# Batched 64x64 matmul: `a` regrouped by its load DMA instead of by a VectorE copy

## The chip, the cores and the metric

The kernel runs on one core of one Trainium2 chip, as one launch with one program. The metric is the device time of that core in microseconds (us), lower is better; each version's time is the median of several runs. The trace comes from one profiled execution, whose own time stands beside the median below.

## The reference

```python
def setup_inputs():
    return {
        "a": np.random.randn(1024, 64, 64).astype(np.float32),
        "b": np.random.randn(1024, 64, 64).astype(np.float32),
    }

def reference(a, b):
    return np.matmul(a, b).astype(np.float32)
```

These are 1024 independent products of a 64x64 matrix `a[i]` with a 64x64 matrix `b[i]`, float32 in and out. Inputs are 16.78 MB each, the output is 16.78 MB.

## The kernel before, in words

The batch is cut into 16 tiles of T = 64 matrices. A matrix of a tile has the index t, h (0 to 3), g (0 to 15). All operands are cast from float32 to bf16 by the DMA that loads them, and all DMAs, loads and stores, are issued from GpSimd (POOL), in one queue and in the order of the code.

- **Load of `a`** (`load_a`, line 59): one DMA a tile fills `a_sb` [128, 4, 8, 64]. Partition (g, mp) holds 8 consecutive rows of `a` (v = 0 to 7) for each h. In DRAM these 8 rows are one run of 8 x 64 float32 = 2 KB; in SBUF they land as one run of 512 bf16 = 1 KB. There are 128 x 4 = 512 such runs a tile.
- **Load of `b`** (`load_b`, line 66): four DMAs a tile, one for each h, put `b` onto the diagonal of a block-diagonal operand `b_bd` [128, 16, 4, 128]: h picks 32 partitions and one of 4 column blocks. Each run is 128 float32 = 512 B in DRAM and 256 B in SBUF, 512 runs a DMA. The zeros off the diagonal are written once, by four VectorE memsets at the start (lines 70 and 76), one for each of the NB = 4 buffers.
- **Regrouping of `a`** (line 88): a VectorE copy reorders `a_sb` (h outside v) to `a_bf` (v outside h), so that the columns (h, k) of one row index v lie together, `a_cols` [128, 8, 256].
- **Transposes** (line 98): 16 TensorE transposes a tile of 128x128 slices of `a_cols` (every second column, by u) into PSUM tiles `at_ps`, and four VectorE copies (line 102) from there to `at_sb`.
- **Products** (line 114): 64 matmuls a tile with 32 columns of `at_sb` as weights and 256 columns of `b_bd` moving, accumulated over u in four PSUM tiles `o_ps`. Each `o_ps` is copied to `o_sb` by ScalarE (line 126) for even gq and by VectorE (line 128) for odd gq.
- **Store** (line 130): one DMA a tile writes 1 MB of `o_sb` (8 KB contiguous a partition) to `out`, where each partition's data are 16 separate runs of 128 float32 = 512 B.

What sets the order: `load_a` and `load_b` run AHEAD = 3 tiles in front of the products, and the store of tile t stands on POOL behind the loads of tile t+3. `a_sb` has 4 buffers, `b_bd` 4, `o_sb` 3, the two PSUM pools 4 each. The DMAs take eight completion semaphores in turn, so that in the program each DMA waits on POOL until the DMA eight places before it has landed, besides its own data waits. A tile issues 6 DMAs: one for `a`, four for `b`, one store.

Of the kernel before, what the change touches and what calls it, by code (L numbers as in the profile page):

```python
# [1 line left out]

# [5 lines left out]

fp32 = mybir.dt.float32
bf16 = mybir.dt.bfloat16  # L10


@with_exitstack
def kernel(
    ctx: ExitStack,
    tc: tile.TileContext,
    a: bass.AP,
    b: bass.AP,
    out: bass.AP,
):  # L20

    nc = tc.nc
    B, M, K = a.shape
    _, _, N = b.shape
    assert (M, K, N) == (64, 64, 64) and B % 64 == 0

    T = 64
    n_t = B // T
    AHEAD = 3
    NB = 4

    a_v = a.rearrange("(t h g) (mp v) k -> t (g mp) h (v k)", h=4, g=16, v=8)
    b_v = b.rearrange("(t h g) (kp u) n -> t h kp g (u n)", h=4, g=16, u=2)
    o_v = out.rearrange("(t hq g4) (mo w) n -> t (g4 mo) hq (w n)", hq=16, g4=4, w=2)

    consts = ctx.enter_context(tc.tile_pool(name="consts", bufs=1))  # L40
    a_pool = ctx.enter_context(tc.tile_pool(name="a_pool", bufs=NB))
    at_pool = ctx.enter_context(tc.tile_pool(name="at_pool", bufs=3))
    o_pool = ctx.enter_context(tc.tile_pool(name="o_pool", bufs=3))
    t_psum = ctx.enter_context(
        tc.tile_pool(name="t_psum", bufs=4, space=bass.MemoryType.PSUM)
    )
    o_psum = ctx.enter_context(
        tc.tile_pool(name="o_psum", bufs=4, space=bass.MemoryType.PSUM)
    )

    b_tiles = []
    for i in range(NB):
        b_bd = consts.tile([128, 16, 4, 128], bf16, name=f"b_bd{i}")
        b_tiles.append(b_bd)
    a_tiles = {}

    def load_a(t):
        a_sb = a_pool.tile([128, 4, 8, 64], bf16, name="a_sb")
        nc.gpsimd.dma_start(  # L59
            out=a_sb[:].rearrange("p h v k -> p h (v k)"), in_=a_v[t]  # L60
        )
        a_tiles[t] = a_sb

    def load_b(t):
        for h in range(4):
            nc.gpsimd.dma_start(  # L66
                out=b_tiles[t % NB][32 * h : 32 * h + 32, :, h, :], in_=b_v[t, h]
            )

    nc.vector.memset(b_tiles[0][:], 0.0)  # L70
    load_a(0)
    load_b(0)
    identity = consts.tile([128, 128], bf16)
    make_identity(nc, identity)
    for i in range(1, NB):
        nc.vector.memset(b_tiles[i][:], 0.0)  # L76
    for t in range(1, AHEAD):
        load_a(t)
        load_b(t)

    for t in range(n_t):
        if t + AHEAD < n_t:
            load_a(t + AHEAD)
            load_b(t + AHEAD)
        a_sb = a_tiles.pop(t)
        b_bd = b_tiles[t % NB]
        a_bf = at_pool.tile([128, 8, 4, 64], bf16, name="a_bf")
        nc.vector.tensor_copy(  # L88
            a_bf[:], a_sb[:].rearrange("p h v k -> p v h k")
        )  # L90
        a_cols = a_bf[:].rearrange("p v h k -> p v (h k)")

        at_sb = at_pool.tile([128, 2, 2, 128, 4], bf16, name="at_sb")
        for w in range(2):
            at_ps = t_psum.tile([128, 4, 2, 128], bf16, name="at_ps")
            for vo in range(4):
                for u in range(2):
                    nc.tensor.transpose(  # L98
                        at_ps[:, vo, u, :], a_cols[:, 2 * vo + w, u::2], identity[:]
                    )  # L100
            for u in range(2):
                nc.vector.tensor_copy(  # L102
                    at_sb[:, w, u, :, :],
                    at_ps[:, :, u, :].rearrange("p vo q -> p q vo"),
                )

        o_sb = o_pool.tile([128, 4, 4, 2, 64], fp32, name="o_sb")
        for gq in range(4):
            o_ps = o_psum.tile([128, 2, 4, 64], fp32, name="o_ps")
            for w in range(2):  # L110
                for u in range(2):
                    for g4 in range(4):
                        g = 4 * gq + g4
                        nc.tensor.matmul(  # L114
                            o_ps[32 * g4 : 32 * g4 + 32, w, :, :],
                            at_sb[:, w, u, 8 * g : 8 * g + 8, :].rearrange(
                                "p mp vo -> p (mp vo)"
                            ),
                            b_bd[:, g, :, 64 * u : 64 * u + 64],
                            start=(u == 0),  # L120
                            stop=(u == 1),
                        )
            dst = o_sb[:, :, gq, :, :]
            src = o_ps[:].rearrange("p w h n -> p h w n")
            if gq % 2 == 0:
                nc.scalar.copy(dst, src)  # L126
            else:
                nc.vector.tensor_copy(dst, src)  # L128

        nc.gpsimd.dma_start(  # L130
            out=o_v[t], in_=o_sb[:].rearrange("p h q w n -> p (h q w n)")
        )


# [1 line left out]
_INS = ['a', 'b']  # L136
_OUTS = [((1024, 64, 64), 'float32')]


# [23 lines left out]
```

## Time and profile before

| | |
|---|---|
| median of 3 runs | 146.64 us (145.87 to 147.1) |
| the profiled execution's own time | 145.87 us |
| its span in the trace | 144.1 us |
| PE busy (with weight loads apart) | 74.8 us, 52% (50.7 us) |
| DVE busy | 86.1 us, 60% |
| ACT busy | 19.2 us, 13% |
| POOL busy, issuing DMAs for nearly all of it | 74.5 us, 52% |
| VectorE regrouping copies (line 88) | 16 of 724 ns |

How to read it: the page gives busy time of each engine, then the span in 40 slices (a digit is a busy share in tenths, 9 for 90% or more), then the DMA queues with packets, bytes and the time that packets took as a share of 16 DMA engines' span (over 100% where packets of one engine overlap). The bytes of a load are counted as they land in SBUF, in bf16, so a 2 KB run of `a` is a packet of 1 KB. Then comes the chain of work that ended last, then the groups of instructions: line, engine, operation, out<-in, count, busy us and mean ns of one, then the idle time of the engine before them and what ended it. A DMA-issuing instruction on POOL is shown as DMA_DIRECT2D; its duration is that of the issuing, not that of the transfer.

### The profile page before, as it was taken

How to read it: one execution, taken by the hardware profiler on the slowest of the kernel's cores; microseconds unless marked ns; L12 is line 12 of the kernel's file. 1: busy time of each engine (PE TensorE's matmuls, PEld its weight loads, DVE VectorE, ACT ScalarE, POOL GpSimd, SP SyncE). 2: the span in 40 equal slices, each digit the busy share in tenths (PEclk: the TensorE clock that was granted, in tenths of full speed). 3: DMA queues.
4: the chain of work that ended last, by engine and by line, in shares of the span. 5: the costliest groups of instructions: out<-in, count | busy, mean ns of one | idle time of the engine just before them, and what ended most of it. 6: DMA issues, size and time to landing. Idle time of an engine off the chain costs nothing.

```text
span 144.1 us, 2993 instructions
## 1 busy us (share of the span) xinstructions
PE 74.8 (52%) x1280; PEld 50.7 (35%) x1280; DVE 86.1 (60%) x116; ACT 19.2 (13%) x33; POOL 74.5 (52%) x102
## 2 busy tenths in 40 slices
PE   0000089786462617558484648829286484856300
PEld 0000057464342414345443325527153354433200
DVE  5777989997776436373565656373463735656300
ACT  3000002231130200202011030301103020110300
POOL 6457881961935627375555738255471655620110
PEclk9999999999999975865559555595557755586855
DMA  1999999999999999999999999999999999999873
GB/s 8 182 177 179 179 178 179 259 187 186 328 209 282 247 228 297 198 321 201 297 234 252 278 210 315 191 309 224 268 256 216 287 207 301 223 284 367 285 232 105
DMA packets 46604, 33.74 MB, mean 234 GB/s; under 512 B 34304, under 2 KB 42496, under 8 KB 46592
## 3 DMA queue, kind: packets, MB, share of 16 engines
q0 software_dynamic: 46592, 33.56, 128.4%
q8 instruction: 10, 0.16, 0.4%
q14 instruction: 2, 0.02, 0.0%
HBM read 33.55 MB, written 16.78 MB: 349 GB/s over the span
## 4 chain that ended last, share of the span: by engine, by line
DMA 52%; DVE 16%; issue 10%; PE 8%; POOL 7%; POOLq 1%; ACT 1%; DVEq 0%
DMA a_sb<-in_a_dram 52%; DVE b_bd L76 7%; PE at_ps L98 5%; POOL out_dram L130 4%; DVE at_sb L102 4%; PE o_ps L114 3%; DVE a_bf L88 3%; DVE b_bd L70 2%; POOL b_bd L66 2%; POOLq L158 1%; ACT o_sb L126 1%; DVE o_sb L128 0%; DVEq L88 0%
## 5 line engine op out<-in xcount | busy, mean ns | idle before, releaser
L66 POOL DMA_DIRECT2D b_bd<-in_b_dram x64 | 42.8, 673 | 42.8 <-DMA a_sb<-in_a_dram 20.4
L114 PE MATMUL o_ps<-b_bd,at_sb 128*32 128x256 bf16 x1024 | 52.7, 359 | 15.2 <-DVE at_sb L102 7.8
L102 DVE COPY at_sb<-at_ps 128x512 bf16<-128x512 bf16 x64 | 39.7, 682 | 11.3 <-PE at_ps L98 11.3
L98 PE MATMUL at_ps<-identity,a_bf 128*128 128x128 bf16 x256 | 22.5, 257 | 44.6 <-DVE a_bf L88 44.6
L114 PEld LDWEIGHTS <-at_sb 128*32 128x32 bf16 x1024 | 31.6, 120 | 33.7 <-DVE at_sb L102 27.8
L128 DVE COPY o_sb<-o_ps 128x512 f32<-128x512 f32 x32 | 21.9, 690 | 26.7 <-DMA out_dram<-o_sb 13.0
L98 PEld LDWEIGHTS <-a_bf 128*128 128x128 bf16 x256 | 19.1, 117 | 50.0 <-DVE a_bf L88 49.3
L126 ACT COPY o_sb<-o_ps 128x512 f32<-128x512 f32 x32 | 17.9, 587 | 114.9 <-DMA out_dram<-o_sb 63.7
L130 POOL DMA_DIRECT2D out_dram<-o_sb x16 | 18.7, 1170 | 19.0 <-issue 7.3
L88 DVE COPY a_bf<-a_sb 128x2048 bf16<-128x2048 bf16 x16 | 11.5, 724 | 7.3 <-DMA a_sb<-in_a_dram 7.2
L59 POOL DMA_DIRECT2D a_sb<-in_a_dram x16 | 12.4, 777 | 0.8 <-POOLq L147 0.8
L76 DVE MEMSET b_bd<- 128x4096 uint32 x3 | 10.4, 3472 | 2.4 <-issue 2.4
L70 DVE MEMSET b_bd<- 128x4096 uint32 x1 | 3.5, 3472 | 1.7 <-PEq L147 1.7
L126 ACT ACT_TABLE_LOAD x1 | 1.3, 1283 | 0.7 <-PEq L147 0.7
masks.py:199 POOL TENSOR_SCALAR_AFFINE_SELECT identity<-identity 128x128 bf16<-128x128 bf16 x1 | 0.3, 313 | 0.1
L147 POOL MEMSET const-float32-0.0<- 128x1 f32 x1 | 0.1, 100 | 0.2 <-issue 0.2
masks.py:197 POOL MEMSET identity<- 128x128 bf16 x1 | 0.2, 224 | 0.0
L147 POOL MEMSET const-bfloat16-1.0<- 128x1 bf16 x1 | 0.1, 103 | 0.0
L147 POOL MEMSET const-uint8-127<- 128x1 uint8 x1 | 0.1, 103 | 0.0
L147 POOL MEMSET const-float32-1.0<- 128x1 f32 x1 | 0.1, 99 | 0.0
## 6 DMA issues: line engine op xcount, KB each, us to landing
out_dram<-o_sb POOLq DMA_DIRECT2D x16, 1024.0 KB, 11.0
a_sb<-in_a_dram POOLq DMA_DIRECT2D x16, 512.0 KB, 12.2
b_bd<-in_b_dram POOLq DMA_DIRECT2D x64, 128.0 KB, 9.4
```

The costliest lines, as they stand in the source:

```text
L59: nc.gpsimd.dma_start(out=a_sb[:].rearrange("p h v k -> p h (v k)"), in_=a_v[t])
L66: nc.gpsimd.dma_start(out=b_tiles[t % NB][32 * h : 32 * h + 32, :, h, :], in_=b_v[t, h])
L70: nc.vector.memset(b_tiles[0][:], 0.0)
L76: nc.vector.memset(b_tiles[i][:], 0.0)
L88: nc.vector.tensor_copy(a_bf[:], a_sb[:].rearrange("p h v k -> p v h k"))
L98: nc.tensor.transpose(at_ps[:, vo, u, :], a_cols[:, 2 * vo + w, u::2], identity[:])
L102: nc.vector.tensor_copy(at_sb[:, w, u, :, :], at_ps[:, :, u, :].rearrange("p vo q -> p q vo"),)
L114: nc.tensor.matmul(o_ps[32 * g4 : 32 * g4 + 32, w, :, :], at_sb[:, w, u, 8 * g : 8 * g + 8, :].rearrange("p mp vo -> p (mp vo)"), b_bd[:, ...
L126: nc.scalar.copy(dst, src)
L128: nc.vector.tensor_copy(dst, src)
L130: nc.gpsimd.dma_start(out=o_v[t], in_=o_sb[:].rearrange("p h q w n -> p (h q w n)"))
L158: with _tile.TileContext(nc) as tc:
```

## The change

`load_a` now does the regrouping itself: `a_sb` is allocated in the order [128, 8, 4, 64] (v outside h), and four DMAs a tile, one for each h, each write a strided [128, 8, 64] part of it. The VectorE copy and its tile `a_bf` go, and the transposes read `a_sb`. The store's source is written as [128, 16, 128] in place of [128, 2048]; destination and data are the same.

```diff
     def load_a(t):
-        a_sb = a_pool.tile([128, 4, 8, 64], bf16, name="a_sb")
-        nc.gpsimd.dma_start(
-            out=a_sb[:].rearrange("p h v k -> p h (v k)"), in_=a_v[t]
-        )
+        a_sb = a_pool.tile([128, 8, 4, 64], bf16, name="a_sb")
+        for h in range(4):
+            nc.gpsimd.dma_start(out=a_sb[:, :, h, :], in_=a_v[t, :, h, :])
         a_tiles[t] = a_sb
...
         a_sb = a_tiles.pop(t)
         b_bd = b_tiles[t % NB]
-        a_bf = at_pool.tile([128, 8, 4, 64], bf16, name="a_bf")
-        nc.vector.tensor_copy(
-            a_bf[:], a_sb[:].rearrange("p h v k -> p v h k")
-        )
-        a_cols = a_bf[:].rearrange("p v h k -> p v (h k)")
+        a_cols = a_sb[:].rearrange("p v h k -> p v (h k)")
...
         nc.gpsimd.dma_start(
-            out=o_v[t], in_=o_sb[:].rearrange("p h q w n -> p (h q w n)")
+            out=o_v[t], in_=o_sb[:].rearrange("p h q w n -> p (h q) (w n)")
         )
```

As compiled, each load of `a` takes 1024 rows of 64 float32 (256 B), which lie one behind the other in DRAM, to 128 x 8 runs of 64 bf16 (128 B), 512 B apart in SBUF. The store compiles to the same 128x16x128 access on both sides in both kernels. A tile now issues 9 DMAs. The load of `a` into a used buffer waits for TensorE's transposes of the tile that lay there, where it waited for the VectorE copy.

## The prediction

> **What bounds the kernel now.** I read the slices first, then the DMA queues, to see whether anything but the DMA engines is full.
>
> ```profile
> DVE  5777989997776436373565656373463735656300
> POOL 6457881961935627375555738255471655620110
> ...
> DMA  1999999999999999999999999999999999999873
> ...
> DMA packets 46604, 33.74 MB, mean 234 GB/s; under 512 B 34304, under 2 KB 42496, under 8 KB 46592
> ...
> q0 software_dynamic: 46592, 33.56, 128.4%
> ...
> HBM read 33.55 MB, written 16.78 MB: 349 GB/s over the span
> ```
>
> The 16 DMA engines are at 9 from the second slice to the last but two, while VectorE and POOL fall to 3 to 7 after the start. So time follows the DMA engines' work. The packets divide into 32,768 of 256 B (`b`: 64 DMAs x 512), 8,192 of 1 KB (`a`: 16 x 512), 4,096 of 4 KB (stores: 16.78 MB / 4 KB) and 1,536 of a few bytes (96 DMAs x 16 completions). The chain of waits and the waits agree:
>
> ```profile
> DMA a_sb<-in_a_dram 52%; DVE b_bd L76 7%; PE at_ps L98 5%; POOL out_dram L130 4%; DVE at_sb L102 4%; PE o_ps L114 3%; DVE a_bf L88 3%; DVE b_bd L70 2%; POOL b_bd L66 2%; POOLq L158 1%; ACT o_sb L126 1%; DVE o_sb L128 0%; DVEq L88 0%
> ```
>
> ```profile
> ACT o_sb L126 <- DMA out_dram<-o_sb: 63.7, 9, 8.1
> ...
> POOL b_bd L66 <- DMA a_sb<-in_a_dram: 20.4, 11, 2.6
> ```
>
> ScalarE waits 63.7 us for stores to free `o_sb`: the arithmetic is ahead of the DMAs. POOL waits 20.4 us until an earlier load lands, the turn of the eight semaphores. In the timeline the loads of `a` are issued at 39.43 and, nine tiles on, at 115.97 us: 8.50 us a tile.
>
> To get a packet's price I asked for the DMA queues in stretches where (nearly) one kind runs: 5 to 7 us (`a`), 10.5 to 12.5 us (`b`), 130.5 to 132.5 us (stores).
>
> ```profile
> DMA packets 418, 0.41 MB, mean 206 GB/s; under 512 B 16, under 2 KB 418, under 8 KB 418
> ```
>
> ```profile
> DMA packets 1436, 0.36 MB, mean 178 GB/s; under 512 B 1436, under 2 KB 1436, under 8 KB 1436
> ...
> q0 software_dynamic: 1436, 0.36, 181.0%
> ```
>
> ```profile
> DMA packets 197, 0.75 MB, mean 375 GB/s; under 512 B 14, under 2 KB 14, under 8 KB 197
> ```
>
> An engine has a sixteenth of each rate. `a`: 206/16 = 12.9 B/ns, so 1,024 B take 80 ns. `b`: 11.1 B/ns, 256 B take 23.0 ns. Stores: 23.4 B/ns, 4,096 B take 175 ns. A tile is 32 x 80 = 2.56, 128 x 23.0 = 2.94 and 16 x 175 = 2.80 us per engine, in sum 8.30; the measured 8.50 leaves 2% for all else. The kernel is bound by packets on the DMA engines.
>
> The issuing side is the second thing to know:
>
> ```profile
> L66 POOL DMA_DIRECT2D b_bd<-in_b_dram x64 | 42.8, 673 | 42.8 <-DMA a_sb<-in_a_dram 20.4
> ...
> L130 POOL DMA_DIRECT2D out_dram<-o_sb x16 | 18.7, 1170 | 19.0 <-issue 7.3
> L88 DVE COPY a_bf<-a_sb 128x2048 bf16<-128x2048 bf16 x16 | 11.5, 724 | 7.3 <-DMA a_sb<-in_a_dram 7.2
> L59 POOL DMA_DIRECT2D a_sb<-in_a_dram x16 | 12.4, 777 | 0.8 <-POOLq L147 0.8
> ```
>
> POOL spends 0.78 + 4 x 0.67 + 1.17 = 4.63 us a tile, 54% of 8.50.
>
> **What the Trainium skill says.** "DMA: Bandwidth & Descriptors", section "Why small descriptors are slow (HBM only)": each packet pays about 3 cycles on the engine's internal bus beside 32 B a cycle, so 256 B cost 11 cycles, 27% of it overhead. The trace agrees in kind: in bytes read, 2,048 B take 80 ns and 512 B take 23.0 ns, a slope of 57/1,536 = 0.0371 ns/B and a constant of 4.0 ns a packet. Same page, "SWDGE vs HWDGE vs iDMA": a packet is at most 4,096 B and may hold several descriptors. The stores show it (4 KB packets from 512 B runs); the loads, which cast, show one packet per run. "Perfetto Trace Analysis", section "DMA Instruction — SWDGE (GPSIMD)": the issuing instruction's window is descriptor generation, not movement; the trace agrees (0.78 us, landing after 12.2). "SBUF — State Buffer", section "Who interferes with whom": a fast VectorE copy can lock GpSimd out of SBUF; the trace shows this at most once (one issue of `b` took 1.105 us beside the copies at 17.9 us, median 0.649).
>
> **The change, part by part.**
>
> *Packets of `a`.* The load no longer moves runs of 2 KB: a run in SBUF is now 64 elements, so one packet reads 256 B and writes 128 B. That is 1,024 x 4 = 4,096 packets a tile where there were 512, 256 an engine in place of 32. The trace has no such packet. The line above gives 4.0 + 256 x 0.0371 = 13.5 ns. Bounds: below, the slope alone, 9.5 ns; above, the 23.0 ns of a `b` packet with twice its bytes. I take 13.5, since the constant fits both loads. A tile's `a` costs 256 x 13.5 = 3.46 us in place of 2.56: +0.90 us, x 16 = +14.4 us (bounds 2.43 and 5.89 us a tile: -2 and +53 us). It lies on the bounding resource from the first load to the last.
>
> *Completions.* 48 more DMAs add 48 small packets an engine, between nothing and about 21 ns each (such packets last about that in the trace): I take +0.5 us, range 0 to 1.
>
> *The VectorE copy.* 16 x 0.724 = 11.6 us go from VectorE, which is 60% busy and waits for DMAs: worth 0, hidden under the transfers. Only the last tile's copy (128.17 us, 0.69 us) is at the end, and behind it ScalarE still waits for a store until 133.7: 0, at best -0.7. At the start the first copy sits behind the memsets, and so does the `at_sb` copy that takes its place.
>
> *Issuing on POOL.* Per tile one issue of 0.777 goes and four come. They hold 1,024 runs each, twice before's. From the store (2,048 runs, 1,170 ns) and the old load (512 runs, 777 ns), both on 128 partitions, a run costs 0.26 ns: 0.777 + 512 x 0.26 = 0.91 us. So 4 x 0.91 + 2.69 + 1.17 = 7.5 us a tile, under the 9.4 us of the DMAs: hidden, cost 0. If the 1,024 rows of the source are each walked like a partition, (777 - 673)/96 = 1.1 ns a row adds about 1 us: 1.88 us an issue. POOL then needs 7.5 + 2.7 + 1.2 = 11.4 us a tile and would bind; the threshold is (9.4 - 3.9)/4 = 1.4 us an issue.
>
> *Fewer bytes in flight.* Eight DMAs in flight were 8/6 of a tile; now 8/9, about 8.3 us of transfers. The first load of `a` landed 5.8 us after its issue, 2.6 of them transfer, so some 3 us of each DMA are latency: the engines do not run dry. The store of tile t waits behind the loads of t+3 as before; if it is late, the loads of t+4 are late, with 8 DMAs still running as cover. New waits of the `a` loads on the transposes of tile t-1 come due before the store of t-1, which stands ahead of them on POOL: 0.
>
> *The store.* The compiled access is the same: 0.
>
> Sum: 144.1 + 14.4 + 0.5 = 159.0 us of span. The profiled run was 1.8 us above its span, the median 2.5: 161 us.
>
> **The rivals.**
>
> 1. *A packet has a floor.* Packets of 41 ns at 23.0 ns spacing (the 181% above, 1.8 at once) and of 98 ns at 80 have the same 18 ns overlap; if only two can be open, a 256 B read (22 + 9.5 = 31.5 ns) can start every 15.8 ns: 4.03 us, +1.47 a tile, 171 us. With a floor at 23.0 ns it is 200. For it: smaller packets are untried here. Against: the constant was 4 ns over a fourfold range.
> 2. *POOL becomes the bound.* At 1.88 us an issue: 64 x 1.88 + 42.8 + 18.7 = 182 us, plus start and the last store's landing (1.3 and 6.5 us) and the launch: 190. For it: the source has 1,024 outer rows. Against: POOL's prices vary little with shape.
> 3. *The reads merge: no slower.* The 1,024 source rows are adjacent, and stores make 4 KB packets of 512 B runs. If the load reads 4 KB at a time and only the writes are cut, `a` costs 16 x 155 to 175 = 2.5 to 2.8 us a tile: -1 to +4 us, 145 to 151, say 147. It decides if the packets of `a` number under 16 x 1,000 or cost under 10 ns. Against: no casting load here shows more than one run a packet, though none had adjacent ones.
>
> **How the numbers follow.** Packet constant, 161 us (its own range 156 to 166): 0.42. Floor, 167 to 200: 0.25. POOL, 167 to 192: 0.20. Merged reads, 145 to 151: 0.13. The range 150 to 190 leaves out most of the merged case and the top of the floor. Slower by over 1% (about what can be told here): the first three and a part of the last, 0.89; within 1%, 0.06; faster, 0.05.
>
> **What would show it.** About 65,536 packets of 128 B, some 30 to 32 ns each; DMA slices at 9 throughout; loads of `a` every 9.4 us of tile; issues of `a` near 0.91 us and POOL busy near 120 us (7.5 x 16); landing of `a` near 8 us; waits of ScalarE on stores still there. Wrong if POOL's row is at 9 and the DMA row is not (rival 2), if 128 B packets come slower than 13.5 ns apart (rival 1), or if there are far fewer of them (rival 3).

## The result, and the profile after

The changed kernel takes 165.48 us (median of 4 runs, 165.29 to 166.58) beside 146.87 us before: 1.131 times as long, 95% interval 1.122 to 1.139. This ratio, like those below, compares the means of undisturbed executions alone: some executions of one and the same kernel run in a slower state, as one of the four of the kernel before did (148.33 us). The profiled execution took 165.47 us, its span is 163.7 us. The prediction was 161 us with a range of 150 to 190; its span was 159.0. The direction and the bounding resource were right. The span came out 4.7 us above the sum, and the experiments show that this small miss hides two larger ones of opposite sign.

The page after, slices and DMA queues:

```profile
POOL 7999997949579667967949388693957949380200
...
DMA  4999999999999999999999999999999999999993
...
DMA packets 104717, 33.75 MB, mean 206 GB/s; under 512 B 100608, under 2 KB 100608, under 8 KB 104704
...
q0 software_dynamic: 104704, 33.56, 166.2%
...
HBM read 33.55 MB, written 16.78 MB: 307 GB/s over the span
```

The DMA row is at 9 from the second slice to the last but one, so the DMA engines still bound the time. The packets grew by 58,113: 57,344 are the load of `a` (65,536 of 128 B where there were 8,192), 768 the completions of 48 more DMAs. The groups and the DMA issues of the same page:

```profile
L60 POOL DMA_DIRECT2D a_sb<-in_a_dram x64 | 55.9, 878 | 3.2 <-DMA a_sb<-in_a_dram 1.5
L65 POOL DMA_DIRECT2D b_bd<-in_b_dram x64 | 41.5, 661 | 22.3 <-DMA out_dram<-o_sb 21.5
...
L121 ACT COPY o_sb<-o_ps 128x512 f32<-128x512 f32 x32 | 17.8, 587 | 133.1 <-DMA out_dram<-o_sb 82.1
L125 POOL DMA_DIRECT2D out_dram<-o_sb x16 | 18.7, 1169 | 13.3 <-DVE o_sb L123 8.5
...
out_dram<-o_sb POOLq DMA_DIRECT2D x16, 1024.0 KB, 8.2
a_sb<-in_a_dram POOLq DMA_DIRECT2D x64, 128.0 KB, 7.8
```

An issue of `a` takes 878 ns, POOL is busy 116.4 us, the arithmetic still waits for stores (ScalarE 82.1 us). One thing is new: POOL waits 21.5 us, at its loads of `b`, for stores to land, where it waited 20.4 us for loads of `a` before. A stretch with almost only packets of `a` (131.8 to 133.8 us) gives their price:

```profile
DMA packets 2405, 0.30 MB, mean 152 GB/s; under 512 B 2405, under 2 KB 2405, under 8 KB 2405
...
q0 software_dynamic: 2405, 0.30, 238.1%
```

16 engines x 2,000 ns / 2,405 = 13.3 ns a packet, 2.4 open at once on each engine. Counted as the prediction counted, from the rate (128 B at 152/16 B/ns), it is 13.5 ns. So far all is as forecast. But the timeline has the stores of tiles 1 and 12 issued at 36.56 and 144.01 us, 9.77 us a tile, where 9.4 was forecast and the kernel before has (122.60 - 29.28)/11 = 8.48. The excess shows where a tile's stores end, here from 70 to 72 us:

```profile
GB/s 420 256 261 502 246 492 164 410 164 410 573 0 410 410 0 410 164 328 164 328 246 164 246 246 246 164 164 82 246 164 164 164 164 246 164 164 82 82 8 187
DMA packets 140, 0.47 MB, mean 237 GB/s; under 512 B 25, under 2 KB 25, under 8 KB 140
```

115 packets of 4 KB take up two whole microseconds, 278 ns an engine and packet where the trace before had 175. In the packet records 373 store packets between 36 us and the last packet of a load took over 250 ns; in the trace before there are 10.

### The profile page after: what moved, and what is told of

The parts are those of the page before. It is cut to its first block, busy times and chain, and to the rows that moved or that the text cites. A ratio compares the mean times of both kernels' runs of the same rounds, so it can differ in the third digit from the quotient of the medians.

```text
span 163.7 us, 3059 instructions
## 1 busy us (share of the span) xinstructions
PE 83.6 (51%) x1280; PEld 58.2 (36%) x1280; DVE 74.7 (46%) x100; ACT 19.1 (12%) x33; POOL 116.4 (71%) x150
## 4 chain that ended last, share of the span: by engine, by line
DMA 63%; POOL 14%; issue 7%; PE 4%; DVE 3%; ACT 3%; POOLq 1%; ACTq 0%; DVEq 0%
DMA out_dram<-o_sb 50%; POOL a_sb L60 8%; DMA b_bd<-in_b_dram 7%; POOL b_bd L65 5%; DMA a_sb<-in_a_dram 5%; PE o_ps L109 4%; ACT o_sb L121 3%; DVE o_sb L123 2%; DVE at_sb L97 1%; POOLq L153 1%; PE at_ps L93 1%; POOL identity masks.py:199 0%; POOL out_dram L125 0%; POOL identity masks.py:197 0%; ACTq L121 0%
## 5 line engine op out<-in xcount | busy, mean ns | idle before, releaser
L109 PE MATMUL o_ps<-b_bd,at_sb 128*32 128x256 bf16 x1024 | 57.4, 395 | 16.0 <-DVE at_sb L97 8.8
L60 POOL DMA_DIRECT2D a_sb<-in_a_dram x64 | 55.9, 878 | 3.2 <-DMA a_sb<-in_a_dram 1.5
L65 POOL DMA_DIRECT2D b_bd<-in_b_dram x64 | 41.5, 661 | 22.3 <-DMA out_dram<-o_sb 21.5
L93 PE MATMUL at_ps<-identity,a_sb 128*128 128x128 bf16 x256 | 26.4, 285 | 53.5 <-DMA a_sb<-in_a_dram 53.5
L109 PEld LDWEIGHTS <-at_sb 128*32 128x32 bf16 x1024 | 35.3, 131 | 35.4 <-DVE at_sb L97 27.7
L93 PEld LDWEIGHTS <-a_sb 128*128 128x128 bf16 x256 | 22.9, 131 | 59.1 <-issue 52.1
L121 ACT COPY o_sb<-o_ps 128x512 f32<-128x512 f32 x32 | 17.8, 587 | 133.1 <-DMA out_dram<-o_sb 82.1
L125 POOL DMA_DIRECT2D out_dram<-o_sb x16 | 18.7, 1169 | 13.3 <-DVE o_sb L123 8.5
```

The lines of the kernel that those rows point to most:

```text
L60: nc.gpsimd.dma_start(out=a_sb[:, :, h, :], in_=a_v[t, :, h, :])
L65: nc.gpsimd.dma_start(out=b_tiles[t % NB][32 * h : 32 * h + 32, :, h, :], in_=b_v[t, h])
L93: nc.tensor.transpose(at_ps[:, vo, u, :], a_cols[:, 2 * vo + w, u::2], identity[:])
L109: nc.tensor.matmul(o_ps[32 * g4 : 32 * g4 + 32, w, :, :], at_sb[:, w, u, 8 * g : 8 * g + 8, :].rearrange("p mp vo -> p (mp vo)"), b_bd[:, ...
L125: nc.gpsimd.dma_start(out=o_v[t], in_=o_sb[:].rearrange("p h q w n -> p (h q) (w n)"))
```

## The experiments

Theory P held that only the price of the 256 B packets counts. Beside it stand theories of the slow store ends: that nine DMAs on eight completion semaphores cause them (S1, later called C, for coupling), that the small packets themselves do (S2), or that each further DMA costs alike (N).

**e1: four DMAs with the old 2 KB runs.**

```diff
-        nc.gpsimd.dma_start(
-            out=a_sb[:].rearrange("p h v k -> p h (v k)"), in_=a_v[t]
-        )
+        for h in range(4):
+            nc.gpsimd.dma_start(
+                out=a_sb[:, h, :, :].rearrange("p v k -> p (v k)"), in_=a_v[t, :, h, :]
+            )
```

> The kernel before with its load of a cut into four DMAs a tile, one for each h, of the same 2 KB runs, and the VectorE copy kept: nine DMAs a tile, no small packets. Theory P (only the price of the 256 B packets counts): 147 us. Theory S1 (of the 19.6 us, 14.7 are packets, and the 4.9 us lost at the ends of stores come from having nine DMAs on eight semaphores, which keeps the engines in step): 151 to 152 us, with stores whose packets take over 200 ns at their ends. Theory S2 (the 4.9 us come from the small packets that follow the store): 147 us. A third theory, that POOL's more numerous issues cost time: over 147 us in the first 30 us of the span.

Measured: 158.34 us, ratio 1.081 (1.075 to 1.086). No theory gave a figure this high. The number of packets is before's (8,192 of 1 KB), yet 11.6 us are lost, and the end of the stores is slow as in the kernel after (507 store packets over 250 ns in mid-span). P alone is refuted: a loss more than half as large as the change's can be had without a single small packet. Nor does the loss lie at the start, as the theory of POOL's issues would have it: from the store of tile 1 to that of tile 12 (35.69 to 135.97 us) a tile takes 9.12 us, where the kernel before has 8.48.

**e2: no copy.** The kernel before without the `tensor_copy` to `a_bf`.

> The kernel before without the VectorE copy at line 88; the transposes read a_sb in the order in which it was loaded, so the regrouping of a is left out of the computation. All theories: 147 us, within 1% of before, since VectorE waits for DMAs; a gain of over 2 us would show that the copy lay on the path.

Measured: 145.47 us, ratio 0.992 (0.989 to 0.995). The copy was worth some 1.2 us, at or above the upper end of the 0 to 0.7 of the prediction, and small beside the 19.6 us by which the span grew.

**e3: one DMA of small packets.**

```diff
-        for h in range(4):
-            nc.gpsimd.dma_start(out=a_sb[:, :, h, :], in_=a_v[t, :, h, :])
+        nc.gpsimd.dma_start(
+            out=a_sb[:], in_=a_v[t].rearrange("p h (v k) -> p v h k", v=8)
+        )
```

> The kernel after with its load of a as one DMA a tile of 4096 reads of 256 B, so small packets with six DMAs a tile as before. P with S1: 160 to 161 us (147 + 14.7 less what the copy gave), stores without slow ends. P with S2: 165 us, slow ends as in the kernel after. If the price were of the DMA count and not of the packets: 147 us. The issue on POOL should take 0.78 + 3584 x 0.26 ns = 1.7 us.

Measured: 156.20 us, ratio 1.065 (1.060 to 1.069), with all 65,536 small packets and six DMAs a tile. The stores are as quick as before (3 packets over 250 ns). The time is below the figures of both theories, 160 and 165 us, so the packets cost less than their price in a stretch of their own. S2 is refuted by the quick stores. The issue took 2,652 ns, not 1.7 us, and POOL at 101.6 us busy still did not bind: the DMA row of this run is at 9 from the second slice to the last but two.

**e4: runs of two rows**, 512 B read, in four DMAs, the copy kept (`a_sb` as [128, 4, 4, 2, 64], each DMA writing `a_sb[:, :, h, :, :]`).

> Four DMAs a tile whose runs are two rows of a, 512 B read and 256 B written, with the VectorE copy doing the rest of the regrouping. P: a packet costs 23.0 ns as those of b, 128 of them 2.94 us a tile in place of 2.56, so +6 us: 153 us. With S1 on top: 158 us. With S2: between 153 and 155 us.

Measured: 158.86 us, ratio 1.084 (1.078 to 1.090), near the 158 us for S1 and the same as e1. The hit is luck: that figure held 6 us for the shorter runs and 5 for the coupling, and e1, with the long runs, already takes 158.34 us. With nine DMAs the run length between 512 B and 2 KB hardly shows.

**e5 and e6: two and three DMAs with 2 KB runs.**

```diff
-        nc.gpsimd.dma_start(
-            out=a_sb[:].rearrange("p h v k -> p h (v k)"), in_=a_v[t]
-        )
+        for lo, hi in ((0, 2), (2, 4)):            # e6: ((0, 2), (2, 3), (3, 4))
+            nc.gpsimd.dma_start(
+                out=a_sb[:, lo:hi, :, :].rearrange("p h v k -> p h (v k)"),
+                in_=a_v[t, :, lo:hi, :],
+            )
```

> The kernel before with its load of a in two DMAs a tile (2 KB runs, copy kept): seven DMAs a tile. With seven, the store of tile t+1 is issued without waiting for the landing of the store of tile t. Theory C (coupling: with eight or nine DMAs a tile on eight semaphores a store, or the load ahead of it, waits until the store before has landed on all 16 DMA engines, so that the engines write their stores at the same time and slowly): 147 to 149 us, stores at about 175 ns a packet in mid-span. Theory N (each further DMA costs alike, by issue, completion or in-flight depth: 11.6 us for three more): 150.6 us, with store packets near 190 ns.

> The same in three DMAs a tile, eight in all: each store waits for the landing of the store before it. Theory C: 156 to 160 us, as with nine, stores over 200 ns a packet on the mean. Theory N: 154.5 us, on a line between 147 and 158.

Measured: 146.43 us for two (ratio 0.999, 0.996 to 1.002), 154.63 us for three (1.052, 1.044 to 1.060). Seven DMAs a tile cost nothing, eight cost 7.6 us, and nine (e1) some 4 us more: a step at eight, not a line. N is refuted by e5, though its figure for e6 (154.5) was the nearer one; C's range for e6 began at 156. The waits show what changes at the step. First e5, then e6, each line giving total us, times and the longest:

```profile
POOL a_sb L60 <- DMA out_dram<-o_sb: 13.5, 11, 1.7
```

```profile
POOL out_dram L132 <- DMA out_dram<-o_sb: 21.5, 10, 2.4
```

In both, POOL waits for a store to land. With seven, it is the first load behind the next store that waits; that next store is already queued. With eight, the next store itself waits; with nine, in the kernel after, the last load of `b` ahead of it:

```profile
POOL b_bd L65 <- DMA out_dram<-o_sb: 21.5, 12, 2.6
```

So from eight on, a store is not issued before the one of the tile before has landed on all 16 engines. Each DMA reports its end 16 times, once for each engine. The traces hold the times of these completions, and the packets one by one. This table sums up mid-span: for the stores of tiles 2 to 12, when a store was issued, counted from the last completion of the store before (a minus is ahead of it), and the time from the first to the last of a store's 16 completions; for the packets, from 36 us to the last packet of a load.

| kernel | DMAs a tile | read run of `a` | ratio | store issued, us | 16 completions within, us | store packets over 250 ns | mean of all, ns |
|---|---|---|---|---|---|---|---|
| before | 6 | 2 KB | 1 | -2.7 | 3.2 | 10 | 172 |
| e5 | 7 | 2 KB | 0.999 | -2.1 | 2.5 | 34 | 173 |
| e6 | 8 | 2 KB | 1.052 | +0.6 | 1.8 | 304 | 197 |
| e1 | 9 | 2 KB | 1.081 | +1.5 | 1.1 | 507 | 216 |
| e4 | 9 | 512 B | 1.084 | +1.4 | 1.3 | 363 | 205 |
| e3 | 6 | 256 B | 1.065 | -2.8 | 2.8 | 3 | 170 |
| e9 | 7 | 256 B | 1.064 | -2.1 | 2.0 | 3 | 170 |
| after | 9 | 256 B | 1.131 | +1.5 | 1.8 | 373 | 203 |

**e7 and e8: stores from SyncE**, `nc.sync.dma_start` for `nc.gpsimd.dma_start` at the store, in the kernel before and in the kernel after.

> The kernel before with its stores issued from SyncE, so in a second ring of each DMA engine and off the eight semaphores of the loads. Writes then mix with reads on every engine. If stores are slow only where all engines write at once: 141 to 146 us, a little under before. If the two rings disturb each other: over 148 us.

> The kernel after with its stores issued from SyncE. The loads keep the 256 B packets and eight DMAs a tile on eight semaphores, with no store among them. Theory C: the part of the loss that comes from coupled stores goes and the packets' part stays, 155 to 159 us. Theory N (the number of DMAs as such): 163 to 166 us.

Measured: 169.20 us (ratio 1.152, 1.145 to 1.159) and 182.09 us (1.240, 1.233 to 1.247). e8 is far above both its figures. e7 lies where it was to lie if the two rings disturb each other, over 148 us, but neither run tests that or the coupling, because the store's packets changed with its queue. The DMA queues of e7:

```profile
q0 software_dynamic: 42240, 16.78, 80.1%
q1 hardware_dynamic: 33024, 16.78, 47.1%
```

From SyncE a store is 32,768 packets of 512 B where GpSimd made 4,096 of 4 KB.

**e9: the kernel after in two DMAs**, one for each half of the partitions.

```diff
-        for h in range(4):
-            nc.gpsimd.dma_start(out=a_sb[:, :, h, :], in_=a_v[t, :, h, :])
+        for lo in (0, 64):
+            nc.gpsimd.dma_start(
+                out=a_sb[lo : lo + 64],
+                in_=a_v[t, lo : lo + 64].rearrange("p h (v k) -> p v h k", v=8),
+            )
```

> The kernel after with its load of a in two DMAs a tile, one for each half of the partitions, in place of four: the same 4096 packets of 256 B, but seven DMAs a tile, so that no store waits for the store before it. Theory C: 156 to 158 us, as with one DMA a tile (156.2), stores near 175 ns a packet. Theory that the small packets themselves slow the stores behind which they come: 162 to 166 us.

Measured: 155.33 us, ratio 1.064 (1.061 to 1.068), a little under the range of theory C and far from the other. The same packets as the kernel after, two DMAs fewer, and 6.7 of its 13.1 per cent are gone: 9.7 us.

**e10 and e11: contiguous stores**, in e1 and in the kernel before. The results then lie in `out` in another order than the reference has.

```diff
-    o_v = out.rearrange("(t hq g4) (mo w) n -> t (g4 mo) hq (w n)", hq=16, g4=4, w=2)
+    o_v = out.rearrange("(t g) (r m) n -> t (g r) (m n)", g=64, r=2)
```

> The kernel of e1 (2 KB runs of a in four DMAs, nine DMAs a tile) with each store written to one contiguous 1 MB of the output, 8 KB a partition, in place of 512 B runs 64 KB apart; the order of the output's elements is left wrong. If the coupled stores are slow because of where the runs fall in memory: the store packets return to about 175 ns and the time to 147 to 150 us. If any store is slow when all engines write at once: 156 to 159 us, as e1.

> The same contiguous store in the kernel before (six DMAs a tile), as the control of e10; the output's order is left wrong. Pattern matters: 142 to 145 us, since the last stores, alone at the end, run faster too. Pattern doesn't matter: 146 to 148 us.

Measured: e10 144.32 us, ratio 0.981 (0.975 to 0.986); e11 140.30 us, 0.961 (0.957 to 0.964). Both ran faster than their ranges. With stores in 512 B runs, four DMAs cost 8.1%; with contiguous stores 0.981 - 0.961 = 2.0% by the ratios and 2.9% by the medians (the four times of e10 scatter from 142.51 to 144.97 us). So two thirds to three quarters of the loss need the scattered stores, although in e10 a store waits as before (it is issued 1.4 us after the landing of the one before). Two things changed at once here: where the runs fall in memory, and the packets, since a contiguous store comes in 2,048 packets of 8 KB where it made 4,096 of 4 KB. Which of the two counts was not tried.

The last stores run with hardly any loads beside them. First the kernel after (150 to 158 us), then e11 (125 to 130 us):

```profile
DMA packets 564, 2.19 MB, mean 274 GB/s; under 512 B 32, under 2 KB 32, under 8 KB 563
```

```profile
DMA packets 333, 2.13 MB, mean 427 GB/s; under 512 B 75, under 2 KB 75, under 8 KB 75
```

The scattered stores go at 274 GB/s there and the contiguous ones at 427. But scattered stores that run alone are not always slow. In e9, from 139.5 to 142.5 us, nothing but stores runs either (282 packets of 4 KB and 19 completions):

```profile
DMA packets 301, 1.16 MB, mean 385 GB/s; under 512 B 19, under 2 KB 19, under 8 KB 301
```

Its store packets take 174 ns, those of the kernel after from 150 to 156.5 us 238. In both stretches one or two more stores are already issued behind the one that is being written. In the kernel before both rates occur: 375 GB/s from 130.5 to 132.5 us, and 279 GB/s for the last store, from 138 to 141 us.

**e12: a version meant to beat both.**

```diff
-    AHEAD = 3
+    AHEAD = 2
...
-        nc.vector.tensor_copy(
+        nc.scalar.copy(
             a_bf[:], a_sb[:].rearrange("p h v k -> p v h k")
         )
```

> A version meant to beat both: the kernel before with the regrouping copy on ScalarE in place of VectorE, and AHEAD = 2 in place of 3. e2 showed 1.2 us for the copy; one store fewer is left for the end, where 256 packets an engine-sixteenth run at 235 ns and not 174, about 1 us. Expected 144 to 146 us; if the loads run dry with the shorter lead, over 147 us.

Measured: 153.94 us, ratio 1.054 (1.050 to 1.059), slower than the kernel before. Its page:

```profile
DMA  1999991999999999999999999999999999999354
GB/s 14 194 173 174 168 114 49 228 179 269 253 239 283 194 316 190 317 201 301 221 264 259 229 293 201 320 190 329 195 320 210 292 233 256 270 223 368 122 145 132
```

The DMA engines run dry in the seventh slice: only three tiles of loads precede the first store, which POOL could not issue before 24.00 us, after 7.44 us idle. At the end they run dry again behind a slower chain, in which ScalarE needs 1,898 ns for the copy (VectorE 724). The two edits were not tried apart. No version that does the whole computation beat the kernel before; e5 equals it.

## Why the prediction was right or wrong

**The bound, and what stays hidden: right.** DMA row at 9, POOL at 71%, issues of `a` at 878 ns (forecast 0.91 us), POOL busy 116.4 us (120), landing 7.8 us (about 8). The rival of a POOL bound falls by the prediction's own sign: it is the DMA row that stays at 9, and POOL's row does not. The rival of merged reads falls with 65,536 packets of 128 B.

**The price of a packet: right by itself.** 13.3 to 13.5 ns against the forecast 13.5; the 238% shows 2.4 packets open, so the rival of a floor at two open packets falls too. What the Trainium skill says in "DMA: Bandwidth & Descriptors", section "Why small descriptors are slow (HBM only)", 11 cycles or 27% overhead for 256 B, fits: at the slope of 0.0371 ns/B 256 B alone are 9.5 ns, so 3.8 of 13.3 ns, 29%, are overhead.

**The term "+0.90 us a tile, +14.4 us": too large.** e9 and e3, the packets without the coupling, cost 6.4 to 6.5%, 9.4 to 9.5 us. Their tiles take 9.00 and 9.05 us by the timelines against 8.48 before, +0.52 to +0.57. They leave out the copy too, which e2 found worth 1.2 us, so the packets alone cost about 10.6 us. The isolated prices would sum to 9.20 a tile for them and to 8.30 for the kernel before: against the measured 9.00 to 9.05 and 8.48 they are 0.2 too high and 0.2 too low. Prices taken from stretches of one kind do not add to better than about 2% where kinds mix, and a forecast of a difference of 0.90 us, a tenth of a tile, stood on just that. Why mixtures with small packets run under their sum is not settled.

**The step "Fewer bytes in flight": this is what failed.** The prediction asked only whether the engines run dry with eight DMAs in flight, found 8.3 us of transfers against 3 us of latency, and costed the loss at 0. A late store, it said, would only make the next loads late, under the cover of the DMAs in flight. As far as the packets tell, the engines hardly ran dry: in mid-span fewer than 16 packets were open for only 1% of the time. But between seven and eight DMAs a tile the semaphores begin to hold a store back until the one before has landed, and store packets get slow: 203 ns on the mean of mid-span in place of 170. About 3,000 such packets on 16 engines make 33 ns x 3,000/16 = 6.2 of the 9.7 us that e9 recovers; where the other 3.5 us lie was not separated. So the change's 13.1% are 6.4% packets, with the copy's gain in them, and 6.7% coupling. The span grew by 163.7 - 144.1 = 19.6 us, and the forecast of 14.4 + 0.5 = 14.9 came near it by luck: the packets' term, with the copy, was 5 us too large, and the coupling, put at 0, costs 9.7.

**The mechanism, as far as shown.** Shown: the step at eight, the wait on the store there, the slow store packets in exactly the kernels beyond it, and that with contiguous stores two thirds to three quarters of the loss are gone. Not shown: why a store that has waited is written slowly. The first idea was that it starts on all 16 engines at about the same time, so that they write without loads in between, while in the kernel before the engines drift apart and stores mix with loads. The traces don't bear this out. In e9 the engines write stores and nothing else for 3 us, at 174 ns a packet. And though the completions of a store do lie closer together in the slow kernels, those of e9 (within 2.0 us, quick) and of e6 and the kernel after (within 1.8 us, slow) are nearly alike. A rival is the smaller depth: eight DMAs in flight are 8/7 of a tile at seven DMAs a tile, one tile at eight, 8/9 at nine. Against it stands that from 70 to 72 us of the kernel after, where the packets are slow, the four loads of `a` behind the store are already issued (66.85 to 70.32 us), and so are one or two more stores in the slow stretch from 150 us on. The wait and the depth change together from seven to eight, so no run tells them apart, and the cause of the slow packets stays open.

**The copy: a little wrong.** Forecast 0, at best -0.7; e2 shows -1.2 us (a gain of 0.7 to 1.6 by its interval).

## What to carry to other kernels

Count a tile's DMAs against the number of completion semaphores before cutting one DMA into several: with as many DMAs a tile as there are semaphores, here eight, each store waited for the store before, and with stores in 512 B runs that cost 5 to 8%, as much as an eightfold number of packets of `a` (6.4%). To try whether a layout change in a load is worth its packets, first give it the same number of DMAs as before, then change the runs. A price per packet from a stretch of one kind is good for ranking; for the difference of two versions it carried an error of some 2% of the whole here.

## What the runs showed of the hardware that had not been expected

- Stores of 512 B runs 64 KB apart, with no loads beside them, ran at 385 GB/s for 3 us in e9 and at 274 to 279 GB/s at the end of the kernels after and before; what decides between the two is open. Stores of 8 KB rows in one contiguous MB reached 427 GB/s (e11) and made the kernel before 3.9% faster, with the output in another order.
- The same store issued from SyncE is cut into 512 B packets, from GpSimd into 4 KB packets, and contiguous from GpSimd into 8 KB packets. With the stores on SyncE the kernel before takes 15% longer; whether by the packets or by the second queue was not told apart.
- Issuing on POOL is not linear in runs: 878 ns for 1,024 runs a DMA, 2,652 ns for 4,096 (e3).
